# First w_o weights asked for late in the branch stage, long scans in pieces of 512 keys, four sums of h one stage sooner, one weight difference on VectorE

## The chip, the cores and the metric

The kernel runs on one core of a Trainium2 chip. A core has a matrix engine (TensorE, PE in the profile), three engines for elementwise work (VectorE or DVE, ScalarE or ACT, GpSimd or POOL), and SyncE (SP), which here only issues DMAs. Each takes its instructions in one fixed order and waits on semaphores for the others. The metric is the device time of one execution in microseconds; the number compared is the median of several executions.

## The reference

A decoder trunk of two layers on 1024 tokens of width 1024, in float32. What matters here is the mixer of each layer:

```python
h = rmsnorm(x, norm1[l])
qa, ka, va, qb, kb, vb, gate_pre = jnp.split(h @ w_in[l], splits, axis=-1)
o_a = dilated_mixture(...)            # 12 heads, three windows and dilations
o_b = stick_breaking_attention(...)   # 4 heads
gates = jax.nn.sigmoid(gate_pre + b_gate[l])
merged = g_a * (o_a @ w_br[l, :OUT_A]) + g_b * (o_b @ w_br[l, OUT_A:])
x = x + merged @ w_o[l]
# stick-breaking, per block of 128 queries:
log_stay = jnp.where(causal, jax.nn.log_sigmoid(-z), 0.0)
later = lax.cumsum(log_stay, axis=3, reverse=True) - log_stay
attn = jnp.where(causal, jnp.exp(jax.nn.log_sigmoid(z) + later), 0.0)
```

A gated ConvFFN follows in each layer; the change does not touch it.

## The kernel before

**Products.** Every float32 operand is split into a high and a low part (`split`, L131 and L136: ScalarE casts the high part, VectorE subtracts it from the source for the low part), and a product is three matmuls, high by high, high by low and low by high (L163 to L165 in `product`, L921 to L923 in `seven`). Some projections are done by a seven-product scheme on 2x2 blocks (`pair`, `seven`), which needs sums and differences of blocks of `h` (`block_sums`, tiles `t_hi`/`t_lo`, sets S[1] to S[4]) and of weight blocks (in `pair`, L1005, L1006, L1010 and L1015).

**Order.** TensorE's order is written out by hand (`manual_schedule` for PE). A class `Dense` holds the projections as generators, and `attend` takes one step of them (two k-tiles, six matmuls) between the pieces of the attention items, so that VectorE and ScalarE have time for the attention's elementwise work. For the other engines a scheduler orders the recorded instructions by a planner's priorities; regions recorded under `high_priority` are put ahead. What is in `dense.side` (the sums of `h`) is taken one entry at a time as soon as the name it waits for is in `done`; when the first seven-product unit starts, what is left there is recorded at once.

**Stick-breaking items.** There are 16 per layer (two pairs of heads, two heads each, four blocks of 256 queries, `qp` 0 to 3). `score` makes for each of two rows of 128 queries the scores of L = 128 to 1024 keys, sigmoids into `beta` (L641) and `stay` (L642), and hands the row to `scans`: a reversed running product over the L keys (L651) and a multiply into `beta` (L654). `turn` transposes four 128x128 blocks of `beta` on TensorE (L667), lowest keys first, and splits the result into `sbh` and `sbl`; `apply` multiplies them with the values (L679). An item has qp + 1 turns; the scores of the next item and their scans run in between. The first turn of an item calls `scans` before its transposes, every turn after them.

**Far items.** `far_item` evicts its scores from the two banks of tag "s" at L826 (VectorE); `pair` runs on TensorE in between, with its weight pieces prepared ahead (w1 to w7; four buffers each for the high and the low parts).

**Branch stage.** After the attention, for 16 steps (eight column blocks of 128, two halves of the tokens), two products with `w_br` go into `br_ps`: the stick-breaking branch in the two banks of tag "t", the dilated one in the two of tag "s". VectorE multiplies each by its gate (L1297; the gates are stored in DRAM as `gs`, loaded as `gin` and put through a sigmoid, L1244) and adds the two (L1302); ScalarE and GpSimd split the sum into the new `h` (L1257, L1258). TensorE's order is branch b of steps 0, 1, 2, then branch a of 0, 1, 2, then both of each further step, so the third product needs the first L1297. In layer 0 four transposes of the residual (L1151) stand behind each step. `branch_in` loads `w_br` for four steps at a time (`br_raw`, 512 KB) and splits it; `wo_chunk` loads `w_o` (two `w_raw` tiles of 256 KB per column block). Both raw tiles, and `u` of `pair`, share two buffers (tag "wr"). The generator `wo[0]` runs as far as its weights with `next(wo[0])`, ahead of the branch loop.

Of the kernel before, what the change touches and what calls it, by code (L numbers as in the profile page):

```python
# [11 lines left out]
ALU = mybir.AluOpType  # L12
# [3 lines left out]
P = 128  # L16
# [40 lines left out]
def trunk_kernel(ctx, tc, x, norm1, w_in, b_gate, w_br, w_o, norm2, w_up, conv_w, conv_b, w_down, norm_f, out, depth=None, probe=None):  # L57
    nc = tc.nc
    act, dve, pe, pool = nc.scalar, nc.vector, nc.tensor, nc.gpsimd
# [15 lines left out]
    zero = cp.tile([P, 1], F32, name="zero")  # L75
# [38 lines left out]
    def bank(tag, name):  # L114
        return ps.tile([P, 512], F32, tag=tag, name=name)
# [338 lines left out]
    def new_s(t):  # L454
        hi, lo = big("t_hi", F32R), big("t_lo", F32R)
        S[t] = [tuple(x.rearrange("p a (b c) -> p (a b) c", c=HF)[:, i, :] for x in (hi, lo)) for i in range(4)]
# [161 lines left out]
    SCANS = []  # L618

    def stick_item(pr, s, qp):  # L620
        if "ob" not in R:
            R["ob"] = big("ob")
        q, k, vt, ob = R["qb", pr], R["kb", pr], R["vb"], R["ob"]
        hd = 2 * pr + s
        rows, st, shared = {}, {}, {}

        def score(a):
            i = 2 * qp + a
            L = P * (i + 1)
            bt = rows[a] = sb.tile([P, T], F32, tag="p4", bufs=4, name="beta")  # L630
            if a == 0:
                st[0] = big("stay")
            sv = st[0][:, a, :]
            for c0 in range(0, L, 512):
                w = min(512, L - c0)
                z = bank("s", "z")
                scores(z[:, :w], *(t[:, s, i * P : i * P + P] for t in q), k[:, s, c0 : c0 + w])
                with tc.high_priority(offset=AHEAD):
                    if c0 + w == L:
                        dve.tensor_tensor(z[:, w - P : w], z[:, w - P : w], mask_b, ALU.add)  # L640
                    act.activation(bt[:, c0 : c0 + w], z[:, :w], AF.Sigmoid)  # L641
                    act.activation(sv[:, c0 : c0 + w], z[:, :w], AF.Sigmoid, scale=-1.0)  # L642
            SCANS.append((bt, sv, L))
            if L <= 512:
                scans()

        def scans():

            for bt, sv, L in SCANS:
                rev = sv[:, 0:L][:, ::-1]  # L650
                one = dve.tensor_tensor_scan(rev, rev, zero[:, 0:1].to_broadcast([P, L]), 1.0, ALU.mult, ALU.add)  # L651
                if "dve" in LAST:
                    tc.add_manual_dep(one.ins, LAST["dve"], NO_SYNC, reason="in turn")
                dve.tensor_tensor(bt[:, 0 : L - 1], bt[:, 0 : L - 1], sv[:, 1:L], ALU.mult)  # L654
            SCANS.clear()

        def blocks(kb):

            return [(j, a) for j in range(2) for a in range(2) if kb + j <= 2 * qp + a]

        def turn(kb):
            if kb == 0:
                scans()
            tp = bank("t", "sb_t")
            todo = blocks(kb)
            for c, (j, a) in enumerate(todo):
                pe.transpose(tp[:, c * P : c * P + P], rows[a][:, (kb + j) * P : (kb + j + 1) * P], ident)  # L667
            shared[kb] = parts(tp, len(todo) * P, "sb")
            scans()

        def apply(kb):
            last = kb == 2 * qp
            if kb == 0:
                shared["o"] = bank("o", "sb_o")[:, :256]
            o = shared["o"]
            for j in range(2):
                c = P if last and j else 0
                for p in (0, 1):
                    pe.matmul(  # L679
                        o[:, c:256],  # L680
                        vt[(kb + j) // 4][:, (kb + j) % 4, hd, :],
                        shared[kb][p][:, 256 * j : 256 * j + 256 - c],
                        start=(kb == 0 and j == 0 and p == 0),
                        stop=(last and j == 1 and p == 1),
                        skip_group_check=True,
                    )
            if last:
                fold(ob[64 * s : 64 * s + 64, pr, qp * 256 : (qp + 1) * 256], o)
                if (pr, s, qp) == (1, 1, 3):
                    nc.sync.dma_start(obd, ob)  # L690

        sc = [lambda: score(0), lambda: score(1)]
        return sc, [(lambda kb=kb: turn(kb), lambda kb=kb: apply(kb)) for kb in range(0, 2 * qp + 2, 2)]
# [233 lines left out]
    def block_sums():  # L927


        keep = {}  # L930

        def first(t, a, b, i):
            if i == 0:
                if "r" not in keep:
                    keep["r"] = quarter("h_sum")
                new_s(t)
            r, (ah, al), (bh, bl) = keep["r"][:, i, :], a()[i], b()[i]
            one = pool.tensor_tensor(r, f32(al), f32(bl), ALU.subtract)
            if "last" in keep:
                tc.add_manual_dep(one.ins, keep["last"], NO_SYNC, reason="one sum after the other")  # L940
            pool.tensor_tensor(r, r, f32(ah), ALU.add)
            keep["last"] = pool.tensor_tensor(r, r, f32(bh), ALU.subtract).ins.name

        def further(t, a, i):
            if t == 4:

                S[4] = half(0, 0)
            elif i == 0:
                new_s(t)
            r, (ah, al) = keep["r"][:, i, :], a()[i]  # L950
            dve.tensor_tensor(r, f32(ah), r, ALU.subtract)
            dve.tensor_tensor(r, r, f32(al), ALU.add)

        def in_two(t, i):
            split(*S[t][i], keep["r"][:, i, :], "waits")

        b11, b12, b21, b22 = (lambda n=n, k=k: half(n, k) for k in range(2) for n in (1, 0))
        todo = []

        def series(after, t, f, lag, gap):  # L960

            at = {}
            for i in range(4):
                at.setdefault(i * gap, []).append(lambda i=i: f(i))
                at.setdefault(i * gap + lag, []).append(lambda i=i: in_two(t, i))
            for k in range(3 * gap + lag + 1):
                todo.append((after, lambda fs=at.get(k, ()): [g() for g in fs]))

        series({"B17"}, 3, lambda i: first(3, b22, b12, i), 6, 4)
        series({"N01s"}, 1, lambda i: first(1, b12, b11, i), 6, 4)  # L970
        series({"N11s"}, 2, lambda i: further(2, b22, i), 1, 1)
        series({"plain"}, 4, lambda i: further(4, b21, i), 1, 1)
        return todo

# [9 lines left out]
    def pair(dense, l, offs, tiled, put):  # L984
# [16 lines left out]
        a11, a12, a21, a22 = (raw[:, i, :] for i in range(4))  # L1001
# [10 lines left out]
        yield  # L1012
        w6 = piece(a11)
        yield
        pool.tensor_tensor(a11, a12, a11, ALU.subtract)  # L1015
        yield
        w3 = piece(a11, "waits")
        u5 = small("u5")
# [135 lines left out]
    def mixer(l, pending):  # L1154
# [80 lines left out]
        todo = [(n, e0 + i) for e0 in range(0, KD, 2) for n in range(2) for i in range(2)]  # L1235
# [25 lines left out]
        wo = [wo_chunk(l, n, e) for n in range(2) for e in range(KD)]  # L1261
# [5 lines left out]
        if l == 0:  # L1267
            for n in range(2):
                new_x(n)
            for h in range(2):  # L1270
                nc.sync.dma_start(X[0][h][:, :, 0:P], xs[0][:, 4 * h : 4 * h + 4, 0:P])
        next(wo[0])
        next(residual, None)

        order = [(i, ab) for ab in (1, 0) for i in range(AHEAD_B)]
# [2 lines left out]
        for i, ab in order:  # L1278
            n, e = todo[i]
            sl = slice(n * HF, (n + 1) * HF)  # L1280
            if i not in seen:
                if e == 0:
                    new_h(n)
                if i % 4 == 0:
                    wb = wbs.pop(0)
                if l and i in X_AT:
                    x_in(X_AT.index(i) // 2, X_AT.index(i) % 2)
            gt = gts[i]
            ec = slice((e % 2) * P, (e % 2 + 1) * P)
            if "ab"[ab] not in oh:  # L1290
                in_two("a")
            o = bank("st"[ab], "br_ps")
            (wh, wl), (xh, xl) = wb[ab], oh["ab"[ab]]
            for _ in product(o, [((wh[:, c, ec], wl[:, c, ec]), (xh[:, c, sl], xl[:, c, sl])) for c in range(2)]):
                pass
            with tc.high_priority(offset=AHEAD):
                dve.tensor_tensor(gt[:, ab, :], gt[:, ab, :], o, ALU.mult)  # L1297
            seen[i] = seen.get(i, 0) + 1
            if seen[i] == 1:
                continue  # L1300
            m = small("mrg")
            dve.tensor_tensor(m, gt[:, 0, :], gt[:, 1, :], ALU.add)  # L1302
            late.append((n, e, m))
            if len(late) > 1:
                merged(*late.pop(0))
            gate_in(i + 3)
            if i % 4 == 1:
                branch_in(i + 3)
            next(residual, None)
        merged(*late.pop(0))  # L1310
        for _ in residual:
# [636 lines left out]
```

## Time and profile before

| | |
|---|---|
| median of 3 runs | 2696.02 us (2694.21 to 2697.93) |
| the profiled execution | 2700.21 us, span 2698.4 us |
| TensorE busy in the span | 2662.5 us (99%), 13104 matmuls |
| VectorE, ScalarE, GpSimd busy | 2017.0, 1352.6, 672.1 us |
| mean granted TensorE clock | 0.997 |
| scan of 1024, 896, 768, 640, 512 keys (L651) | 2284, 2024, 1748, 1489, 1225 ns, 8 of each |
| its multiply (L654), 1023, 895, 767, 639, 511 keys | 1223, 1083, 958, 825, 687 ns, 8 of each |
| weight difference on GpSimd (L1015) | 1291 ns median, 20 of them |

How to read it. A matmul row's length holds the pipeline's latency; what a matmul costs is the distance from its start to the next one's, 0.23 us for 128x512 at the full clock. So the gap shown before a matmul that waited is some 0.16 us less than what it cost. The profile of the layers: stick-breaking items at about 73 to 237 us and 1407 to 1571 us, near items to 336 and 1670, far items to 569 and 1903, the branch stage to about 625 and 1959, then `w_o` and the FFN.

### The profile page before, as it was taken

The numbers are of one execution on the slowest core, as the hardware profiler recorded it, in microseconds if no ns is written. First come the engines' busy times: TensorE is split into PE (matmuls) and PEld (weight loads), VectorE is DVE, ScalarE is ACT, GpSimd is POOL, SyncE is SP. The second block draws the span as 40 slices with busy tenths as digits, with TensorE's granted clock in tenths as the row PEclk, the third lists the DMA queues.
The fourth block names the chain that finished last, engine by engine and source line by source line (L and its number), as shares of the span: only waits on it lengthen the run. The fifth ranks groups of instructions, "written<-read, shape, count | busy, mean of one in ns | idle before, by whom it ended". The sixth has DMA issues, their size and how long they took to land.

```text
span 2698.4 us, 36609 instructions
## 1 busy us (share of the span) xinstructions
PE 2662.5 (99%) x13104; PEld 2233.0 (83%) x13104; DVE 2017.0 (75%) x2974; ACT 1352.6 (50%) x2494; POOL 672.1 (25%) x487
## 2 busy tenths in 40 slices
PE   9999999999999999999999999999999999999999
PEld 8988888878888888888888888888788888888888
DVE  5776855675788888897657777566858888898865
ACT  5655645474455555532435565455645555554225
POOL 1003221122233444321210042211211443343210
PEclk9999999999999999999999999999999999999999
DMA  5012178663234444688411122785732444446863
GB/s 161 28 56 85 57 189 247 199 231 105 82 124 166 146 151 150 222 319 319 161 36 43 48 79 87 210 247 177 233 89 76 156 156 141 164 149 252 330 248 120
DMA packets 358689, 421.03 MB, mean 156 GB/s; under 512 B 20732, under 2 KB 287340, under 8 KB 356972
## 3 DMA queue, kind: packets, MB, share of 16 engines
q1 hardware_dynamic: 358508, 418.70, 47.0%
q8 instruction: 103, 1.69, 0.3%
q14 instruction: 78, 0.64, 0.1%
HBM read 278.59 MB, written 140.05 MB: 155 GB/s over the span
## 4 chain that ended last, share of the span: by engine, by line
PE 84%; DVE 8%; issue 2%; ACT 2%; DMA 2%; POOL 0%; SPq 0%; DVEq 0%; ACTq 0%; POOLq 0%
PE u_a L921 5%; PE u_a L922 5%; PE u_a L923 5%; PE d_ps L1644 5%; PE d_ps L1645 5%; PE d_ps L1646 5%; PE u_c L921 3%; PE u_c L922 3%; PE u_c L923 3%; PE i_a L921 2%; PE i_a L922 2%; PE i_a L923 2%; PE o_ps L163 2%; PE o_ps L164 2%; PE o_ps L165 2%
## 5 line engine op out<-in xcount | busy, mean ns | idle before, releaser
L136 DVE TENSOR_TENSOR w_lo<-up_a,w_hi 128x512 fp32r<-128x512 f32 x240 | 237.6, 996 | 20.6 <-ACT w_hi L131 20.6
L131 ACT CAST w_hi<-up_a 128x512 fp32r<-128x512 f32 x240 | 149.3, 622 | 184.1 <-PE u_a L922 45.3
L1652 DVE TENSOR_TENSOR x<-x,d_ps 128x512 f32<-128x512 f32 (+1 forms) x228 | 151.8, 671 | 76.6 <-PE d_ps L1646 75.3
L1383 POOL TENSOR_TENSOR cv<-cv 128x512 f32<-128x512 f32 x88 | 132.3, 1515 | 249.3 <-DVE cv L1378 139.5
L136 DVE TENSOR_TENSOR w_lo<-w_raw,w_hi 128x512 fp32r<-128x512 f32 x148 | 111.6, 757 | 61.9 <-ACT w_hi L131 61.3
L136 DVE TENSOR_TENSOR g<-cv,g 128x512 fp32r<-128x512 f32 x154 | 152.6, 992 | 5.2 <-ACT g L131 2.7
L131 ACT CAST w_hi<-w_raw 128x512 fp32r<-128x512 f32 x148 | 91.9, 621 | 125.3 <-PE o_ps L164 64.3
L131 ACT CAST w_hi<-in_a 128x512 fp32r<-128x512 f32 x120 | 74.6, 621 | 121.1 <-PE i_c L922 53.6
L136 DVE TENSOR_TENSOR w_lo<-in_a,w_hi 128x512 fp32r<-128x512 f32 x120 | 86.8, 723 | 61.9 <-ACT w_hi L131 61.5
L1644 PE MATMUL d_ps<-gd_in,w_hi 128*128 128x512 f32 (+1 forms) x340 | 130.4, 384 | 1.7 <-issue 0.9
L1646 PE MATMUL d_ps<-gd_in,w_lo 128*128 128x512 f32 (+1 forms) x340 | 129.8, 382 | 0.0
L1645 PE MATMUL d_ps<-gd_in,w_hi 128*128 128x512 f32 (+1 forms) x340 | 129.8, 382 | 0.0
L921 PE MATMUL u_a<-hh,w_hi 128*128 128x512 f32 x320 | 124.6, 389 | 0.8 <-DVE u L1534 0.8
L922 PE MATMUL u_a<-t_lo,w_hi 128*128 128x512 f32 x320 | 124.5, 389 | 0.0
L922 PE MATMUL u_a<-hl,w_hi 128*128 128x512 f32 x320 | 124.5, 389 | 0.0
L923 PE MATMUL u_a<-hh,w_lo 128*128 128x512 f32 x320 | 124.5, 389 | 0.0
L921 PE MATMUL u_a<-t_hi,w_hi 128*128 128x512 f32 x320 | 124.5, 389 | 0.0
L923 PE MATMUL u_a<-t_hi,w_lo 128*128 128x512 f32 x320 | 124.5, 389 | 0.0
L1644 PE MATMUL d_ps<-gd_in,wd 128*128 128x512 f32 (+1 forms) x292 | 113.9, 390 | 0.0
L131 ACT CAST g<-cv 128x512 fp32r<-128x512 f32 x154 | 94.9, 616 | 37.2 <-POOL cv L1383 29.9
L1646 PE MATMUL d_ps<-gd_in,wd 128*128 128x512 f32 (+1 forms) x292 | 112.8, 386 | 0.0
L1645 PE MATMUL d_ps<-gd_in,wd 128*128 128x512 f32 (+1 forms) x292 | 112.8, 386 | 0.0
(404 smaller groups left out, 8606.7 us busy)
## 6 DMA issues: line engine op xcount, KB each, us to landing
gd<-g SPq DMA_DIRECT2D x154, 512.0 KB, 3.7
gd_in<-gd SPq DMA_DIRECT2D x154, 512.0 KB, 5.9
up_a<-in_w_up_dram SPq DMA_DIRECT2D x80, 512.0 KB, 4.9
t_kq<-tk SPq DMA_DIRECT2D x32, 768.0 KB, 4.7
wd_raw<-in_w_down_dram SPq DMA_DIRECT2D x22, 1024.0 KB, 11.8
w_raw<-in_w_in_dram SPq DMA_DIRECT2D x80, 256.0 KB, 3.0
in_a<-in_w_in_dram SPq DMA_DIRECT2D x40, 512.0 KB, 5.4
gin<-gs SPq DMA_DIRECT2D x32, 512.0 KB, 4.1
```

What stands on the lines that cost most here:

```text
L131: one = act.copy(hi, src)
L136: two = dve.tensor_tensor(lo, src, f32(hi), ALU.subtract)
L163: pe.matmul(o, lh, rh, start=(first and i == 0), stop=False, skip_group_check=share)
L164: pe.matmul(o, lh, rl, start=False, stop=False, skip_group_check=share)
L921: pe.matmul(o, w[0][:, c], rh, start=(first and i == 0), stop=False, skip_group_check=True)
L922: pe.matmul(o, w[0][:, c], rl, start=False, stop=False, skip_group_check=True)
L923: pe.matmul(o, w[1][:, c], rh, start=False, stop=(last and i == 3), skip_group_check=True)
L1383: return lambda: pool.tensor_tensor(dst, a, b, ALU.subtract)
L1644: pe.matmul(o[:, sub], wh[:, c], gh[:, sub], start=(i == 0 and k in (0, 4, 5)), stop=False, skip_group_check=True)
L1645: pe.matmul(o[:, sub], wh[:, c], gl[:, sub], start=False, stop=False, skip_group_check=True)
L1646: pe.matmul(o[:, sub], wl[:, c], gh[:, sub], start=False, stop=(i == m - 1), skip_group_check=True)
L1652: dve.tensor_tensor(x, x, o[:, sub], ALU.add)
```

## The change

Four edits, both layers:

- `next(wo[0])` moves from ahead of the branch loop into it, behind its step 12 (of 0 to 15).
- `score` hands a row to `scans` in pieces of at most 512 keys, highest keys first; a piece's scan starts from the last value of the piece above it. A turn takes all but two of the pieces that wait (at least one) instead of all; the first turn of an item still takes all.
- In `block_sums`, the four sums that make S[2] (`less`, formerly part of `further`) wait for "N01s", no longer for "N11s", and their splits follow at once when "N11s" is there.
- In `pair`, the difference a12 - a11 (L1015) is taken on VectorE.

```diff
-            SCANS.append((bt, sv, L))
+            for c1 in range(L, 0, -512):
+                SCANS.append((bt, sv, max(0, c1 - 512), c1, L))
             if L <= 512:
                 scans()
-        def scans():
-            for bt, sv, L in SCANS:
-                rev = sv[:, 0:L][:, ::-1]
-                one = dve.tensor_tensor_scan(rev, rev, zero[:, 0:1].to_broadcast([P, L]), 1.0, ALU.mult, ALU.add)
+        def scans(most=9):
+            while SCANS and most:
+                most -= 1
+                bt, sv, c0, c1, L = SCANS.pop(0)
+                rev = sv[:, c0:c1][:, ::-1]
+                one = dve.tensor_tensor_scan(rev, rev, zero[:, 0:1].to_broadcast([P, c1 - c0]), 1.0 if c1 == L else sv[:, c1 : c1 + 1], ALU.mult, ALU.add)
                 if "dve" in LAST:
                     tc.add_manual_dep(one.ins, LAST["dve"], NO_SYNC, reason="in turn")
-                dve.tensor_tensor(bt[:, 0 : L - 1], bt[:, 0 : L - 1], sv[:, 1:L], ALU.mult)
-            SCANS.clear()
+                k0, k1 = max(0, c0 - 1), c1 - 1
+                dve.tensor_tensor(bt[:, k0:k1], bt[:, k0:k1], sv[:, k0 + 1 : k1 + 1], ALU.mult)
...
             shared[kb] = parts(tp, len(todo) * P, "sb")
-            scans()
+            scans(max(1, len(SCANS) - 2))
...
             if t == 4:
                 S[4] = half(0, 0)
-            elif i == 0:
-                new_s(t)
+            less(a, i)
+
+        def less(a, i):
             r, (ah, al) = keep["r"][:, i, :], a()[i]
...
-        series({"N11s"}, 2, lambda i: further(2, b22, i), 1, 1)
+        for i in range(4):
+            todo.append(({"N01s"}, lambda i=i: less(b22, i)))
+        series({"N11s"}, 2, lambda i: i or new_s(2), 0, 1)
...
-        pool.tensor_tensor(a11, a12, a11, ALU.subtract)
+        dve.tensor_tensor(a11, a12, a11, ALU.subtract)
...
-        next(wo[0])
         next(residual, None)
...
             if i % 4 == 1:
                 branch_in(i + 3)
+            if i == 12:
+                next(wo[0])
             next(residual, None)
```

## The prediction

> **What bounds the kernel now.** The page's first part, then who waited for whom on TensorE.
>
> ```profile
> PE 2662.5 (99%) x13104; PEld 2233.0 (83%) x13104; DVE 2017.0 (75%) x2974; ACT 1352.6 (50%) x2494; POOL 672.1 (25%) x487
> ...
> PE br_ps L163 <- DVE gin L1297: 8.0, 4, 3.7
> PE sb_o L679 <- DVE sbl L136: 4.3, 4, 1.7
> PE o L743 <- DVE p0l L136: 2.7, 3, 1.2
> ...
> PE z L599 <- DVE st L826: 2.4, 3, 1.4
> ```
>
> TensorE is busy all but 36 us, so the change can win only from those waits (columns: sum, times, longest). The instruction order of the changed program, engine by engine, has TensorE's 13071 built instructions in the same order as before: its work is unchanged, and a stall can only shrink, grow or move. From start to start a stall costs 0.16 us or so more than its gap (front table), so I use starts below. The four rows above are then 8.8 + 5.6 + 3.5 + 3.8 = 21.7 us.
>
> The largest, in layer 1, in TensorE's, ScalarE's and VectorE's timelines, then busy time by engine of two short stretches (the column behind POOL's is the granted clock):
>
> ```profile
> 1905.99 0.39 PE L165 MATMUL br_ps<-oh_b,br_w 128*128 128x512 f32 x1
> 1910.05 0.50 PE L163 MATMUL br_ps<-oh_b,br_w 128*128 128x512 f32 x1 [3.66 <-DVE gin L1297]
> ...
> 1911.38 0.63 PE L164 MATMUL br_ps<-ol_b,br_w 128*128 128x512 f32 x1
> 1911.80 0.63 PE L165 MATMUL br_ps<-oh_b,br_w 128*128 128x512 f32 x1
> ...
> 1906.92 0.62 ACT L131 CAST w_hi<-w_raw 128x512 fp32r<-128x512 f32 x1 [5.55 <-DMA w_raw<-in_w_o_dram]
> 1908.57 1.33 ACT L1244 ACTIVATE gin<-gin,bg 128x512 f32<-128x512 f32 x2
> ...
> 1904.02 1.05 DVE L903 TENSOR_TENSOR on<-on,jn 128x512 f32<-128x512 f32 x1
> 1907.57 0.69 DVE L136 TENSOR_TENSOR w_lo<-w_raw,w_hi 128x512 fp32r<-128x512 f32 x1 [2.50 <-ACT w_hi L131]
> 1909.31 1.28 DVE L1297 TENSOR_TENSOR gin<-gin,br_ps 128x512 f32<-128x512 f32 x2
> ...
> 576.20:579.50 3.30, 3.30 (x12) 2.62 (x10) 1.29 (x2) 0.00 (x0) 0.00 (x0) 0.50 0.51 176
> 1910.70:1914.10 3.40, 3.40 (x10) 2.61 (x9) 0.69 (x1) 0.78 (x3) 0.00 (x0) 0.50 1.02 343
> ```
>
> L1297 was ready at 1905 and stood on VectorE behind a w_o split whose DMA (issued 1899.72) came at 1906.9. And the wait costs twice: after it the matmuls start 0.427 us apart, not 0.23, at granted clock 0.50, for 3.4 us. The only other half-clock stretch after the kernel's start and ahead of its end follows the 2.52 us gap at 572.09 in layer 0.
>
> **Part 1, w_o late.** Moved: two DMAs of 256 KB on SP's queue, two casts (ACT, 0.62) and two subtractions (DVE, 0.69) per layer. On SP they leave the place ahead of the `br_raw` load of steps 4 to 7 (and of two `gs` stores and two gate loads); that `br_raw`, 512 KB, takes their buffer at about 555 and 1889 instead of 567 and 1909. Their own new place is behind all four `br_raw`, and there a late buffer would hold up gate loads on SP and gate sigmoids on ACT.
> Layer 0 loses: the stall, start to start 571.70 to 574.61 less the pitch of 0.23, 2.68; then six slow matmuls and the slow transposes behind them, 6 x 0.197 + 0.6 = 1.8; together 4.4. What is late next: VectorE's order has two `br_w` subtractions (0.6 apart) in place of the two `w_lo`, already split on ACT by 566, so the first L1297 ends at about 571.5 against a need at 571.95; then the third gate's sigmoid (done 574 to 575.3) feeds the sixth product at 576.8, about even. I keep 0.2: minus 4.2.
> Layer 1 loses 3.82 + 7 x 0.197 = 5.2. Next: the first L1297 follows L903 and one `br_w` (1905.02 + 0.6), ends 1906.3, need 1906.22: 0.1. Then the third gate load, issued 1900.56: its neighbour issued 1902.35 took 7.65 us, so it lands at about 1908.2, sigmoids end near 1909.6, two L1297 later 1910.8 against the sixth product's need at 1910.4: 0.4. Late in the stage VectorE has 29.95 us of 32 busy at 1925 to 1957 (TensorE's waits there 0.68 + 0.18 + 1.41, start to start); the two `br_w` leave its early half (minus 0.7), two `w_lo` join its last steps, 1.4 us with 0.2 us of room per step: plus 1.0. Minus 4.4. In layer 0 VectorE has 25.12 of 32 busy, which covers them; without that cover 1.4 to 3.5 (two `w_lo`, 0.69 to the 1.72 of one at 604.51). Together **minus 8.6**, bounds minus 10.5 (nothing is late next) to minus 4 (half of each stall stays and the clock still drops).
>
> The Trainium skill (TensorE: Matmul & The Clock Gate, "HAM oscillation") gives the rule for the clock as no idle gap over about 3.4 us. Here a gap of 2.52 us was followed by the half clock, so the trace does not keep that threshold; by the page layer 0's drop would have another cause and stay, and the sum would be 1.8 us smaller.
>
> **Part 2, scans in pieces.** 32 rows over 512 keys get one scan and one multiply more. From the rows: (2284 - 1225)/512 = 2.07 ns a key, so a scan has 0.17 us fixed; the multiply (1223 - 687)/512 gives 0.15. 32 x 0.32 = 10.2 us more on VectorE, hidden: it is busy 49.78 of 65 us at 85 to 150.
>
> ```profile
> 143.25 2.29 DVE L651 TENSOR_TENSOR_SCAN stay<-stay,zero 128x1024 f32<-128x1024 f32 x1 [0.56 <-ACT stay L642]
> 145.57 1.23 DVE L654 TENSOR_TENSOR beta<-beta,stay 128x1023 f32<-128x1023 f32 x1
> 146.71 0.68 DVE L136 TENSOR_TENSOR w_lo<-w_raw,w_hi 128x512 fp32r<-128x512 f32 x1
> 147.32 1.15 DVE L136 TENSOR_TENSOR sbl<-sb_t,sbh 128x512 fp32r<-128x512 f32 x2
> ```
>
> TensorE wanted the first of these `sbl` at 146.12 and got it at 148.06: 1.94. In the new order that `sbl` stands behind the first piece: 143.25 + 1.23 + 0.69 + 0.6 (w_lo) + 0.6 = 146.4, a wait of 0.35. The like stall at 235.01 (0.61) goes. Against it: the first turn needs the lowest keys, which are the last piece, so a row is ready 0.32 us later, more where other work is let in. The one first turn already late (198.30, 0.46, beta ending 198.24) gets to 1.05, and that at 136.55 (beta ending 134.89) has a second piece, its multiply and a pulled-in `sbl` to take: 0.1. The others keep room (109.64 against 108.13; 223.37 against 220.73). Per layer minus 1.6 - 0.6 + 0.6 + 0.1 = minus 1.5; layer 1 shows the same stalls (1.94, 0.60, 0.46): **minus 3.0**, bounds minus 6.0 (all gone) to plus 3 (each of the 16 long items 0.5 late).
>
> The Trainium skill (VectorE: DVE Perf Modes, "The TRN2 errata") speaks against cutting: a fixed latency is paid once per instruction; with its 58 cycles at 0.96 GHz I estimate 64 x 0.06 = 3.9 us for the added ones. The trace has 10.2; by either it is VectorE time under cover.
>
> **Part 3, sums sooner.** `p0l` waits at 329.99 and 333.19 (0.66, 1.30) and 1663.6, 1666.8 (0.32, 1.33). ScalarE's cast of `p0h` stood behind casts of the last sums, which waited for VectorE; VectorE's `p0l` stood behind steps of the same sums. The new order has three 0.6 us steps fewer ahead of the first `p0l` (two split subtractions and two sum steps out, the weight difference in) and `p0h` one cast behind the sums instead of three: `p0l` ready at about 328 and 330.8 against 329.3 and 331.3. Late next is `w_lo` of piece w3, now behind them (about 332.0 against 331.9). Minus 1.8 and minus 1.5, less 0.3 each: **minus 2.7**, bounds minus 3.6 to plus 1.5 (w3's split 1 us later in both layers).
>
> **Part 4, difference on VectorE.** GpSimd loses 20 x 1.29, VectorE gains 20 x 0.69 = 13.8 us (that is L1010's 692 ns, same form) in stages where it is busy 58 of 104 and 77 of 120 us. At 453.57 L1015 took 1.84, ScalarE's cast waited for it to 455.44, VectorE's split waited for that with L826 behind it, TensorE 1.53. In layer 1 the same place waits 0.99 with L1015 done early, for the buffer that TensorE frees: so 0.55 is to be had, and 20 more steps of 0.6 can push a `p1l` late (TensorE waited for one six times, 0.3 to 0.9): plus 0.25. **Minus 0.3**, bounds minus 2.5 to plus 3.
>
> **Sum.** Minus 8.6, 3.0, 2.7, 0.3: minus 14.6. The profiled execution took 2700.2 (span 2698.4), so 2685.6 for one like it; the median of the runs lies 4.2 lower, so 2681.4.
>
> **Rivals.**
> *A new wait in the branch stage.* The gate load at 1908 and its like in layer 0 hold the sixth product longer, or `br_raw`, twice `w_raw`'s bytes in a stretch where loads took 7.65 us, comes late to an ACT cast with gates behind it: half of part 1 is lost, 4.3, and another us of clock: 2686.7. For it: DMA share 0.79 there. Against: `br_raw` is asked for 11 us before its need.
> *Given back at the stage's end.* The moved `w_lo` cost TensorE their worst length, 1.78 (one at 1940.52) each: 4 x 1.78 = 7.1 less the 1.0 counted: 2687.5. For: VectorE 94% busy there in layer 1. Against: 78% in layer 0.
> *Slower: rows late to their first turn.* If the limit on pieces leaves the last piece to the next turn, every long item's first transposes wait. Rooms per layer are 1.5, 3.0, 1.7, 3.3, none, 1.9, 2.6, 3.0 us; a row later by 0.3 plus one turn (3.6 us) overruns them by 14.3, twice 28.6. With the other parts, plus 17: 2713. It decides from a delay of about 3.3 us a row; the new order has at most one split of the running item between a row's two pieces, 0.6 us and not a turn, which speaks against.
> *It does not do what it says.* The stalls pass to the next instruction in line, engines even: 2696. Against: the stage where most is to be had waits for one DMA.
>
> **How the numbers follow.** Forecast 0.62, branch wait 0.16, given back 0.10, no effect 0.06, slower 0.06. About 0.2% (5.4 us) is what can be told from no change. Faster by more: the first three less a few = 0.84; within: 0.10; slower: 0.06. Range: the forecast's terms give 2675 to 2687, widened to the two partial cases and the deeper bounds: 2674 to 2691.
>
> **What would show it.** Right: no TensorE wait on L1297 over 1 us in the branch stage's first 8 us, no half clock after the start, `sbl` waits under 0.5, `p0l` waits gone, first-turn wait near 1.0 in the 13th item of both layers. Wrong: a gap over 2 us at `br_ps` on ACT or DMA; gaps at `sb_t` spread over the long items; TensorE waits on L1297 of 1 us and more at the stage's end.

## The result, and the profile after

The changed kernel takes 2682.5 us (median of 4 runs, 2682.0 to 2682.6) where the kernel before takes 2697.0 beside it (2694.2 to 2698.4): a ratio of 0.9947, 95% interval 0.9930 to 0.9964, so 14.5 us or 0.5% faster. The forecast was 2681.4. The profiled execution took 2681.95 (span 2679.8).

The page's first part and then who waited for whom on TensorE (columns: sum, times, longest), the changed kernel:

```profile
PE 2657.5 (99%) x13104; PEld 2231.1 (83%) x13104; DVE 2027.9 (76%) x3058; ACT 1352.1 (50%) x2494; POOL 641.9 (24%) x467
...
PE sb_t L671 <- DVE beta L659: 1.8, 2, 0.9
...
PE z L599 <- DVE st L830: 1.3, 2, 0.6
PE br_ps L163 <- DVE gin L1303: 1.0, 2, 0.8
```

Lines have moved by 4 to 8: L659 is the multiply that was L654, L830 the eviction L826, L1303 the gate multiply L1297. The rows on `sbl` (4.3) and `p0l` (2.7) are gone, the one on the gate multiply went from 8.0 to 1.0, and one row has grown, the transposes that wait for `beta`. In the kernel before it was

```profile
PE sb_t L667 <- DVE beta L654: 0.5, 2, 0.2
```

VectorE has 10.9 us more work.

The beginning of layer 1's branch stage, VectorE's timeline and then busy time by engine (behind POOL's column the granted clock), the changed kernel:

```profile
1892.07 1.09 DVE L907 TENSOR_TENSOR on<-on,jn 128x512 f32<-128x512 f32 x1
1893.06 0.70 DVE L136 TENSOR_TENSOR br_w<-br_raw,br_w 128x512 fp32r<-128x512 f32 x1
1893.66 0.70 DVE L1303 TENSOR_TENSOR gin<-gin,br_ps 128x512 f32<-128x512 f32 x1
...
1891.00:1899.00 8.00, 8.00 (x36) 6.28 (x35) 6.36 (x10) 3.78 (x6) 0.00 (x0) 1.00 0.82 288
```

The first gate multiply follows `on` (the old L903) and one `br_w` split, with nothing waited for between; TensorE is busy 8.00 of 8 us at the full clock, where it stood 3.66 us and then ran 3.4 us at half.

In both traces all 13104 matmuls stand in one order, so the start of the same matmul in both can be compared at the end of each stage. After minus before, what each stage added (us):

| stage | layer 0 | layer 1 | the part that acts there | forecast, both |
|---|---|---|---|---|
| stick-breaking items | -1.90 | -1.99 | 2, scans | -3.0 |
| near items | -1.70 | -1.44 | 3, sums | -2.7 |
| far items | -0.05 | -1.00 | 4, difference | -0.3 |
| branch stage | -3.91 | -6.48 | 1, w_o | -8.6 |

With 0.1 at the start and -0.3 in what follows that is -18.6. It is more than the 14.5 between the medians; the profiled execution before was a long one (2700.2), and the experiments show which waits vary from one execution to the next.

### The profile page after: what moved, and what is told of

Read it like the earlier page. It is cut to its first block, busy times and chain, and to the rows that moved or that the text cites. A ratio compares the mean times of both kernels' runs of the same rounds, so it can differ in the third digit from the quotient of the medians.

```text
span 2679.8 us, 36678 instructions
## 1 busy us (share of the span) xinstructions
PE 2657.5 (99%) x13104; PEld 2231.1 (83%) x13104; DVE 2027.9 (76%) x3058; ACT 1352.1 (50%) x2494; POOL 641.9 (24%) x467
## 3 DMA queue, kind: packets, MB, share of 16 engines
q8 instruction: 103, 1.69, 0.3%
## 4 chain that ended last, share of the span: by engine, by line
PE 89%; DVE 6%; ACT 1%; issue 1%; DMA 1%; POOL 0%; DVEq 0%; SPq 0%; ACTq 0%; POOLq 0%
PE u_a L925 5%; PE u_a L927 5%; PE u_a L926 5%; PE d_ps L1652 4%; PE d_ps L1654 4%; PE d_ps L1653 4%; PE i_a L925 3%; PE u_c L927 3%; PE u_c L926 3%; PE u_c L925 3%; PE i_a L926 3%; PE i_a L927 2%; PE o_ps L163 2%; PE o_ps L164 2%; PE o_ps L165 2%; PE g_ps L163 2%
## 5 line engine op out<-in xcount | busy, mean ns | idle before, releaser
L655 DVE TENSOR_TENSOR_SCAN stay<-stay,zero 128x512 f32<-128x512 f32 (+2 forms) x96 | 93.5, 974 | 28.8 <-ACT stay L642 28.2
L1652 PE MATMUL d_ps<-gd_in,wd 128*128 128x512 f32 (+1 forms) x292 | 113.9, 390 | 0.0
L1654 PE MATMUL d_ps<-gd_in,wd 128*128 128x512 f32 (+1 forms) x292 | 112.8, 386 | 0.0
```

Source lines behind the costliest of these rows:

```text
L1652: pe.matmul(o[:, sub], wh[:, c], gh[:, sub], start=(i == 0 and k in (0, 4, 5)), stop=False, skip_group_check=True)
L1654: pe.matmul(o[:, sub], wl[:, c], gh[:, sub], start=False, stop=(i == m - 1), skip_group_check=True)
```

## The experiments

Single edits first, then single edits undone, then variants. The kernel before ran beside each group: 2694.7 (35 runs, experiments 1 to 4), 2697.2 (9, 5 to 8), 2695.8 (9, 9 to 12), each on a chip of its own; over all these runs it lies between 2691.1 and 2700.3. Experiment 8's kernel ran in the second and the third group and links them: the changed kernel is 2.0 above it. The ratios are estimated from all runs and differ by up to 0.0004 from the quotients of the medians.

**1. The first edit alone.**

```diff
-        next(wo[0])
         next(residual, None)
...
+            if i == 12:
+                next(wo[0])
```

> Before with the first edit alone (w_o asked for behind step 12 of the branch loop). Theory, parts add up: both stalls of TensorE on the first L1297 of the branch stage go with the half clock behind them; TensorE gains 4.0 us in layer 0 and 5 to 6.5 us in layer 1 over the stage, the median falls by 8.6 (7 to 10). With it goes what varies in the kernel before: its runs lie 4.2 us apart, and if that is the arrival of the w_o load and the length of the half clock behind it, the runs of this kernel lie within 1 us. Rival, the stage gives it back without the other edits (a br_raw or gate load late in its place): a gap of over 1 us at br_ps stays, the median falls by under 5. Rival, the spread has another source: this kernel's runs lie 3 us or more apart.

2690.3 (2689.1 to 2692.3, 11 runs): 4.3 less than before, ratio 0.9988 (0.9979 to 0.9996). Both stalls at the first gate multiply and the half clocks behind them are gone (branch stage -4.1 and -6.8 in the trace), yet the median moves by less than half of that and misses the 7 to 10 that were expected. The rival for a fall under 5 was a gap of over 1 us left at `br_ps`; the trace has none, the longest wait there is 0.70. And the runs still lie 3.2 apart: the theory on what varies holds only a part. The trace has the other one: at 1786.38 a wait of 1.53 for L826, and a half clock behind it. Experiment 5 takes that up.

**2. The second edit alone** (the two hunks of `score` and `scans` and the one of `turn`, as in the diff above).

> Before with the second edit alone (scans in pieces of 512 keys). Theory: the waits of sb_o on sbl of 1.9 and 0.6 us go in both layers, the first turn of the 13th item waits 1.1 us where it waited 0.46, nothing else moves; TensorE gains 1.9 us per layer over the stick-breaking items, the median falls by 3 to 4. Rival, the earlier arrival shifts the transfers of the branch stage and part of it is lost there: under 2. As the two stalls of the branch stage stay, the runs should still lie 3 us or more apart.

2691.9 (2687.0 to 2695.8, 12 runs): 2.7 less, where 3 to 4 was expected, ratio 0.9989 (0.9981 to 0.9998). The items end 1.96 and 1.94 earlier, the 1.9 and 0.6 waits on `sbl` are gone, the first turn of the 13th item waits 1.10 in both layers (from start to start, like the other waits below): as expected, place by place. Runs 8.8 apart, as the branch stalls stay.

**3. The third edit alone** (the two hunks of `block_sums`).

> Before with the third edit alone (four sums of h one stage sooner). Theory: the p0l waits (0.66 and 1.30 in layer 0, 0.32 and 1.33 in layer 1) go, one wait of 0.2 us on w_lo comes in each layer; TensorE gains 1.5 us per layer, the median falls by 2.5 to 3. Rival, those waits went in the changed kernel because the weight difference left GpSimd or the items ahead ended sooner: they stay here, and the median falls by under 1. Runs 3 us or more apart, as the branch stalls stay.

2691.2 (2688.4 to 2695.4, 11 runs): 3.5 less, ratio 0.9989 (0.9981 to 0.9998). All four `p0l` waits are gone without the other edits, and the near items end 1.69 and 1.42 earlier in the trace. The rival is out.

**4. The fourth edit alone.**

```diff
-        pool.tensor_tensor(a11, a12, a11, ALU.subtract)
+        dve.tensor_tensor(a11, a12, a11, ALU.subtract)
```

> Before with the fourth edit alone (a12 - a11 on VectorE). Theory, from the changed kernel's trace: the z wait at 457 of layer 0 shrinks by 0.7, waits on p1h and p1l at about 518 and 559 grow by 0.5 each, layer 1 gains 0.6 to 1.2 at the z waits; together minus 0.8 to minus 1.4. Rival, this gain belongs to the order that the sums leave behind them: the z waits stay as they are, and the median moves by less than 0.5. Runs 3 us or more apart, as the branch stalls stay.

2693.4 (2689.8 to 2694.8, 11 runs): 1.2 less, ratio 0.9993 (0.9984 to 1.0002). The `z` waits are 0.80 in both layers, as in the changed kernel, so the rival is out, though the interval reaches past no change. Not all of the gain comes from there: of the four `p0l` waits two are gone and two are 1.08, 1.2 us less in all, a gain that the third edit makes without this one. Of the waits that were expected to grow, one did, on `p1h` at 516 (0.41).

The four medians add up to -11.8, against -13.6 (experiment 9) and -14.5 for all together: medians of such spreads tell no difference there, and each part shows its effect in the trace without the others.

**5. The fourth edit undone.**

> The changed kernel with the fourth edit undone (a12 - a11 back on GpSimd). Theory, the fourth edit takes away a wait of varying length: the z wait at about 453 and 1779, 0.8 in the changed kernel, is 0.98 in some layers and executions and 1.53 in others, and a 1.53 can be followed by a half clock of 3.41 us where it falls into one 3.41 us window; the runs lie 1.5 us or more apart, where the changed kernel's lay 0.6 apart, and the median is 0.8 to 2 above 2682.5. Rival, only the trace's difference of 1.4 us counts: median 2683 to 2684 and runs within 0.8 us. Rival, worth nothing as forecast (0.3): median within 0.5 of 2682.5.

2685.0 (2683.4 to 2686.0, 5 runs), 2.6 above the changed kernel's first median, and 5.0 above experiment 8 beside it, so 3.0 above the changed kernel that way; the forecast's price was 0.3, and 0.8 to 2 was expected here. The place in layer 1, in GpSimd's, VectorE's and TensorE's timelines and a stretch behind it:

```profile
1775.94 1.84 POOL L1022 TENSOR_TENSOR in_a<-in_a 128x512 f32<-128x512 f32 x1 [16.63 <-DVE w_lo L136]
...
1775.94 0.69 DVE L1076 TENSOR_TENSOR u<-u,kq_h 128x512 fp32r<-128x512 f32 x1
...
1779.55 0.33 PE L599 MATMUL z<-t_kq 128*128 128x128 f32 x1 [1.36 <-DVE st L830]
...
1781.00:1784.40 3.40, 3.40 (x11) 2.71 (x10) 0.66 (x4) 1.82 (x5) 2.24 (x2) 0.50 0.84 224
```

And the same place in layer 0 of the same execution:

```profile
450.01 1.30 POOL L1022 TENSOR_TENSOR in_a<-in_a 128x512 f32<-128x512 f32 x1 [17.08 <-DVE w_lo L136]
...
450.02 1.83 DVE L1076 TENSOR_TENSOR u<-u,kq_h 128x512 fp32r<-128x512 f32 x1
...
453.08 0.33 PE L599 MATMUL z<-t_kq 128*128 128x128 f32 x1 [0.82 <-DVE st L830]
```

GpSimd's difference and VectorE's L1076 start within 0.01 us of each other. In layer 0 GpSimd's takes 1.30 and VectorE's 1.83 instead of 0.69; in layer 1 VectorE's takes 0.69 and GpSimd's 1.84: one goes, and the other takes longer by nearly the first one's time (1.14 for 1.30 in layer 0, 0.54 for 0.69 in layer 1). If GpSimd loses, the weight piece is 0.54 later and TensorE's wait at `z` is 1.53 from start to start, not 0.98, and in layer 1 a half clock follows. In the five traces with the difference on GpSimd that is ten such places: six waits of 0.97 to 0.98 and four of 1.52 to 1.53, three of these with a half clock behind. In all nine with it on VectorE (18 places) the wait is 0.80 with no half clock. The Trainium skill (SBUF — State Buffer, "Who interferes with whom") gives the rule: VectorE with two inputs in SBUF and a GpSimd instruction that reads SBUF share a port pair under an exclusive lock, and issue order decides who blocks. The traces agree, with 1.83 against 0.69 and 1.84 against 1.30.

**6. The first edit undone.**

> The changed kernel with the first edit undone (w_o asked for ahead of the branch loop). Theory, the first edit is worth what single edits showed, 4.3 us in the median, though the profiled execution of before held 10 us of it: the stall on the first L1297 is 2.5 to 3 us in layer 0 and anything from 1.5 to 4 us in layer 1, with a half clock behind some; median 2686 to 2689, runs 3 us or more apart. Rival, the forecast's 8.6 for the median: 2690 to 2692.

2686.7 (2684.2 to 2688.2, 5 runs), 4.2 above the changed kernel's first median, 6.7 above experiment 8 and so 4.7 above the changed kernel that way: about the price of experiment 1. Two waits at the first gate multiply, 2.87 and 2.80 from start to start, and no half clock behind either. TensorE's wait in layer 1, and busy time in and after it:

```profile
1897.88 0.50 PE L163 MATMUL br_ps<-oh_b,br_w 128*128 128x512 f32 x1 [2.64 <-DVE gin L1304]
...
1898.00:1902.00 4.00, 4.00 (x18) 3.27 (x19) 2.11 (x4) 1.85 (x4) 0.00 (x0) 1.00 1.03 336
```

So the wait of the first edit comes in several sizes. In five traces that have it, it is 2.66 to 2.93 in layer 0 and 1.54, 2.47, 2.80, 3.82, 3.96 in layer 1, and 6 of the 10 have a half clock behind them. The load of the second `w_raw` sets the size: from its issue to its cast on ScalarE (issued 1899.72, cast 1906.92 in the kernel before) it takes 4.18 to 4.45 in layer 0 and 4.91 to 7.32 in layer 1, and in all ten places the wait is that time less 1.52 to 1.55 in layer 0, less 3.36 to 3.38 in layer 1. Both layers together they cost from 5.7 us (this execution) to some 10 (experiment 2's, with both half clocks); the execution that the forecast was made from had 9.6. The medians, 4.3 alone and 4.7 undone, lie below even the least of these; the interval of experiment 1 (1.1 to 5.7 us) just reaches it, and where the rest goes is not shown.

**7. Two more sums on VectorE.**

```diff
-        pool.tensor_tensor(u2, a11, a21, ALU.subtract)
-        pool.tensor_tensor(a21, a21, a22, ALU.add)
+        dve.tensor_tensor(u2, a11, a21, ALU.subtract)
+        dve.tensor_tensor(a21, a21, a22, ALU.add)
```

> The changed kernel with the two other weight sums of pair on VectorE too (a11 - a21 and a21 + a22). Theory, what the fourth edit gains comes from GpSimd no longer running beside VectorE's splits: at 510 of layer 0 a w_lo split took 1.52 us beside these two sums where 0.69 is usual, and the p1h and p1l waits at 513.4 and 514.0 (0.57 and 0.48) and at 554.7 and 555.3 (0.38 and 0.48) follow; with the sums on VectorE they shrink by 0.4 to 1 in all, median 0.5 to 1.5 below the changed kernel's. Rival, 40 more steps of 0.6 us on VectorE push p1l and L830 late: 0.5 to 2 above it.

2682.1 (2678.3 to 2682.9, 5 runs), 2.1 above experiment 8 beside it, as the changed kernel is: nothing gained. The theory and its rival each hold at one place: the `w_lo` split at 510 takes 0.69 (it took 1.52) and the waits behind it at 513 and 514 shrink by 0.83; but at 1808 the two sums stand ahead of a `p1l` on VectorE and TensorE waits 0.68. Of the two waits only the second (0.47) also stands in the changed kernel's other trace (experiment 9), so the 0.83 is not to be had in every execution.

**8. The 13th item's rows whole.**

```diff
-            for c1 in range(L, 0, -512):
-                SCANS.append((bt, sv, max(0, c1 - 512), c1, L))
+            most = L if (pr, s, qp) == (1, 0, 2) else 512
+            for c1 in range(L, 0, -most):
+                SCANS.append((bt, sv, max(0, c1 - most), c1, L))
```

> The changed kernel with the rows of the 13th stick-breaking item (second pair, first head, rows of 640 and 768 keys) scanned whole, as before. Theory: the first-turn wait of 1.10 at 197 and 1523 goes back to 0.46, no sbl wait of 1 us comes for it, TensorE gains 0.64 per layer: 1.3 below the changed kernel, 2681.2. Rival, the whole scans of 1.7 us put an sbl late as they did at 148: nothing gained, 2682.5 or above.

2680.0 (2679.4 to 2681.7, 5 runs). The waits at 196 and 1521 are 0.45 again, the items end 0.6 earlier in both layers than with the cut, no `sbl` comes late. The traces account for 1.2 of the 2.0 by which this kernel is faster; the rest is not explained. With the row of 768 keys whole, scan and multiply end 4.02 us after the scan's start (192.40 to 196.42); in two pieces of each, with the same two steps of `ql` between, 4.66 (192.53 to 197.19), 0.21 of it for a mask step (L640) that now stands between the pieces.

**9. The changed kernel again, 10. the last one again, on one chip.**

> The changed kernel itself, to have it beside the next two on one chip. Theory (what varied in the kernel before was the wait for w_o and the wait behind the weight difference, each with a half clock behind it at times): the runs lie within 1 us, 2681.5 to 2683. Rival, the first four runs lay close by chance: 2 us or more apart.

2682.2 (2681.0 to 2683.5, 5 runs). The runs lie 2.5 apart, not 1: the rival is nearer; kernels with both edits still vary, by less than the 8.0 of the kernel before.

> The 13th item's rows whole once more, now beside the changed kernel on one chip. Theory: 1.3 us below it, 2680 to 2681.3. Rival, the first difference (2680.0 against 2682.5) was the chip: within 0.4 us of the changed kernel.

2680.2 (2679.1 to 2680.5, 5 runs), 2.0 below the changed kernel beside it, and no run of the one in the range of the other. This version beats both: 0.9942 of before (0.9929 to 0.9954).

**11. w_o behind step 4.**

```diff
-            if i == 12:
+            if i == 4:
                 next(wo[0])
```

> The changed kernel with w_o asked for behind step 4 of the branch loop, not 12. In the instruction order the two loads then stand on SyncE behind the last gate store and ahead of the br_raw loads of the later steps. Theory, two things count, the splits must stand behind the first gate multiplies on VectorE and the loads must not hold the two buffers that br_raw needs: the first wait stays away, but a br_raw comes late and TensorE waits 1 to 3 us at br_ps around step 4 to 8 of both layers; median 2684 to 2687. Rival, only the place behind the first gate multiplies counts: median within 0.7 of the changed kernel's and no wait over 1 us in that stretch.

2686.9 (2684.6 to 2689.5, 5 runs), 4.7 above the changed kernel beside it. The first gate multiply is on time, and TensorE waits later instead. SyncE's queue and TensorE's wait in layer 0:

```profile
566.87 0.93 SPq L148 DMA_DIRECT2D w_raw<-in_w_o_dram  x2
572.62 1.57 SPq L1257 DMA_DIRECT2D br_raw<-in_w_br_dram  x2
574.42 3.35 SPq L1249 DMA_DIRECT2D gin<-gs  x3
577.87 0.38 SPq L1153 DMA_DIRECT2D xr<-in_x_dram  x1
...
584.31 0.63 PE L1158 MATMUL x_t<-ident,xr 128*128 128x128 f32 x4 [3.01 <-DMA xr<-in_x_dram]
```

In the changed kernel the `br_raw` loads went out at 567.94; here the first waits until 572.62 for a buffer that w_o holds (its `w_lo` split ends at 572.60), and the queue behind it waits too. The victim in layer 0 is not `br_raw`, which was expected, but the residual's `xr`, issued 4 us later than in the changed kernel (573.88). In layer 1 the waits are 1.28 and 0.31 at 1903 and 1905: a `w_lo` split, late itself, stands ahead of the third gate multiply on VectorE. So a place behind the first gate multiplies is not enough.

**12. Experiment 8 with experiment 7 in layer 0 only.**

> The 13th item's rows whole, and in layer 0 alone the two other weight sums of pair on VectorE. Theory, from the traces: 0.6 per layer from the first, 0.4 to 0.8 in layer 0 from the second (the waits on p1h and p1l at 513 and 555, where a w_lo split ran slow beside GpSimd), none of the 0.68 that those sums cost at 1808 in layer 1: 1.7 to 2.1 below the changed kernel, 2680.0 to 2680.8. Rival, the waits at 513 and 555 differ from execution to execution anyway (0.57 and 0.48 in the changed kernel, 0 and 0.48 in the one with the 13th item whole): no more than that kernel gains, 1.3.

2680.2 (2679.6 to 2681.2, 5 runs), the same as experiment 10. The median lies in the range of the theory, but nothing was gained over experiment 10: the wait at 512 (0.47 there) is gone, and at 482 the two sums stand ahead of a `p1l` on VectorE and TensorE waits 1.08. So the rival has the outcome (no more than that kernel gains), though not for its reason.

## Why the forecast held

**The sum.** 2681.4 forecast, 2682.5 measured. But two errors cancel in it, so that the number came this close is in part luck. The gain in the profiled execution was 18.6, not 14.6; and the 4.2 us by which the medians lay below that execution were carried over to the changed kernel, whose profiled execution lies 0.5 below its own median. The waits of the first edit, long and with both half clocks in that execution, are the likely cause that it was a long one, and the change removes them.

The total of 21.7 us with which the prediction opens is too high: read from start to start, the waits of its four rows are 8.6, 5.1, 3.5 and 2.9, some 20. No term of the sum rests on it.

**Part 1, minus 8.6.** The mechanism was right to the detail: at the first gate multiply 0.14 is left in layer 0 and 0.11 in layer 1 (0.2 and 0.1 foreseen), and no half clock. The term was mis-sized in layer 1. The failing step is "plus 1.0" late in its stage: the `w_lo` splits that joined it cost nothing that can be seen. TensorE's waits over 0.2 there sum to 0.9 to 2.5 in eight traces with w_o late (mean 1.6) and to 0.7 to 2.4 in five with w_o early (mean 1.7). The two profiled executions drew 2.1 before and 1.35 after, and the 0.4 kept for the third gate's sigmoid left no wait over 0.15; this brings the term to -10.4 for them. For the medians it is -4.3 to -4.7 (experiments 1 and 6), half of the forecast: the load's arrival and the half clock vary, and the profile had drawn a long wait in layer 1 and both half clocks.

**Part 2, minus 3.0**, came as -3.9 in the trace and -2.7 in the median. The 1.94 wait left nothing, where 0.35 was kept for it: the new order, in VectorE's timeline of the changed kernel, has

```profile
143.17 1.22 DVE L655 TENSOR_TENSOR_SCAN stay<-stay,zero 128x512 f32<-128x512 f32 x1
144.43 0.69 DVE L659 TENSOR_TENSOR beta<-beta,stay 128x512 f32<-128x512 f32 x1
145.03 0.68 DVE L136 TENSOR_TENSOR w_lo<-w_raw,w_hi 128x512 fp32r<-128x512 f32 x1
145.64 0.68 DVE L136 TENSOR_TENSOR sbl<-sb_t,sbh 128x512 fp32r<-128x512 f32 x1
146.24 1.27 DVE L655 TENSOR_TENSOR_SCAN stay<-stay,zero 128x512 f32<-128x512 f32 x1
```

with `sbl` between the two pieces. The 13th item waits 1.10 (1.05 foreseen) and the other items nothing: the rival of late rows had no place but that one.

**Part 3, minus 2.7**, came as -3.1 in the trace and -3.5 in the median; the wait on w3 is 0.18, 0.29 with the next matmul's slow start, for 0.3 kept.

**Part 4, minus 0.3**, was mis-sized: -1.0 in the trace, -1.2 in the median alone (`p0l` waits included) and -2.6 to -3.0 when undone. The step that failed is "In layer 1 the same place waits 0.99 with L1015 done early", from which it took that "0.55 is to be had": 0.99 was the short outcome of a race between two engines, 1.53 in layer 0 the long one, and either layer may draw either; a half clock that the profile had not drawn was not counted. The 0.25 for more `p1l` waits is not told apart from what varies there (0 to 0.57 at 513).

**The rivals.** In the changed kernel no wait over 0.15 stands in the first 14 us of either branch stage, nothing was given back at their ends, and no first turn but the 13th's is late.

## What to carry to other kernels

When the profiled execution is longer than the median, ask which of the waits that you are about to price made it so, and price them from several traces: here they halved this change's largest term, from 8.6 to between 4.3 and 4.7 in the medians. Two elementwise operations, one on VectorE and one on GpSimd, that start together on two inputs each went in either order here (6 to 4 in ten places), with different waits behind them; putting both on one engine removed 1 to 3 us where one trace promised 0.3. A load moved late has to clear both what it delayed on the engines and the buffers and the queue that the next loads need: step 4 of 16 lost in its queue what step 12 won.

## What the hardware showed that was not expected

VectorE's rows add up to 15.0 us more (2168.5 to 2183.5), though the scans and multiplies took 11.8 more (10.2 foreseen) and the differences 14.4: its other steps got 11.2 shorter. The 16 steps of L1069 (L1076 in the changed kernel), which the race in experiment 5 can hold up, went from 14.3 to 11.0 in all.

The half clock does not follow a length of gap. In each trace its stretches begin on one grid of 3.413 us: 9.49, 576.10, 1910.71 and 2695.78 in the kernel before are 166, 391 and 230 steps apart, and each inner one lasts 3.41 us. What fits the traces is the time that TensorE loses inside one step of the grid (start to start, less the median distance for a matmul of its shape): of the steps that lost over 2.4 us, five of five were followed by a half clock; between 1.8 and 2.2, four of ten; under 1.8, none (14 traces, the start and the end of the kernel left out). What decides between 1.8 and 2.2 stays open. So the gap of 1.36, with the slow starts of small matmuls around it (experiment 5), brought one, while 2.87 and 2.80 us from start to start (experiment 6; 1.41 + 1.46 and 1.09 + 1.71 on the two sides of a grid line) and 3.17 (experiment 11; 1.75 + 1.42) did not. The Trainium skill (TensorE: Matmul & The Clock Gate, "Part 1: The HAM clock gate") states a free-running window of 3413 ns, and the traces agree with that; its rule of a whole idle window, about 3.4 us, they do not keep. That the phase of this grid against the program changes from execution to execution (2.66, 0.56, 2.11 us from the span's start in three kernels) would explain why the same wait costs some 1.6 us more in one execution and nothing more in another; the traces show it place by place, not for the runs without a trace.
